# An encoder layer on one core: x loads from two queues, sines behind the Squares, token 512 split once, even sums begun in the second k loop, operand loads behind gate loads

## Chip, cores and metric

The kernel runs on 1 core of one Trainium2 chip. The metric is the device time of one execution in microseconds, given as the median of several runs. A profiled execution has its own time and its own span, which is counted from the first to the last instruction.

## What is computed

Two sequences (x_prompt and x_sample, each 1024 tokens x 1024 channels) go through one layer. Cut to what matters:

```
xn = rmsnorm(x, g_pre);  p = xn @ w_in
fv, fg, hv, hg, mg = split(p)                       # 1024, 1024, 3072, 1024, 2048 columns
fz = fftn(fv as (L, 4 groups, 256), axes=(L, 256)).real
y_f = (fz * silu(fg)) @ w_fourier_out
v, x1, x2 = split(short_conv(hv, w_short))          # width 3 along the sequence
kf = rfft(two-sided filters from a small MLP with two sines)
z = v
for n, gate in enumerate((x1, x2)):
    z = gate * (long_conv(z, kf[:, n]) + hyena_d[n] * z)
y_h = (z * silu(hg)) @ w_hyena_out
g_f, g_h = split(sigmoid(mg + b_merge))
out = (g_f * y_f + g_h * y_h) @ w_out
return x + rmsnorm(out, g_post)
```

Everything is float32. TensorE multiplies rounded operands (F32R), so each operand is split into a rounded part h and a remainder l, and one product is three matmuls: h x h, h x l and l x h (`mm3`). The rounding is a ScalarE cast, the remainder a VectorE (or GpSimd) subtraction; both together are `split`.

## The kernel before

The kernel has four phases in order of time: the Fourier phase (0 to about 225 us), the main phase with filters, input projections and long convolutions (to about 1700 us), the gates, and the output phase (from about 1990 us). Each engine executes its instructions in order. That order comes from a tile scheduler that goes by priorities, by the buffers of the pools (tiles with one tag share `bufs` buffers, and a new tile waits until the readers of the old one are done) and by explicit constraints: `tc.issue_after(ins)` puts what is issued in its block behind the instruction `ins`, where both are on the same engine. DMAs started with `nc.sync`, `nc.scalar` and `nc.gpsimd` are issued from the queues of SyncE (SP), ScalarE (ACT) and GpSimd (POOL).

`phase_fourier` goes through the sequences b = 0 and b = 1.

- `hidden(layer, px, pf)` (L273) computes one layer of the filter network: a matmul `phd`, a chain of VectorE operations that brings the argument into the range of the sine (`sin_of`, L256), two Sin activations on ScalarE, and the store of the result. Layer 0 is called ahead of the first sequence; layer 1, which reads layer 0 back, behind the last half.
- `norm(b, px, pf)` (L303) loads eight tiles x (128 tokens x 1024 channels) on SP, squares each on ScalarE with a row sum, takes the reciprocal root for four tiles at a time in eleven small VectorE operations (`rstd`) and makes four diagonal matrices `dg` from it. For b = 1 it is placed behind the last rounding of the second half's weights (`behind`).
- `xtile(b, k, px, fo)` (L327) is one step of the k loop over the 128-channel blocks: matmuls `tpx` against the diagonals transpose and normalise block k; ScalarE copies them to `xg`, scaled with g_pre; `xg` is stored to `d_x`. VectorE folds the tokens (`eo`, even and odd parts; the odd part of b = 1 is on GpSimd), and `eh`, `el` are their split. Token 512, which has no partner in the fold, is split in every step with two VectorE operations of 128 x 2 (`x5`). Tile xg has two buffers, and GpSimd writes its two last columns with a memset.
- `weights(pw, W, half, k, first)` (L360) loads the block `wfv` of the input projection's Fourier columns on SP, adds and subtracts its halves (`wer`, `wor`) and splits them (`we`, `wo`).
- `pfv(p, e, m, k, W, fo)` is one step over k of sum m of the even (e = 0) or odd (e = 1) part. For b = 0 six of the eight sums of the first half are begun: their PSUM tiles are allocated ahead of the k loop (four in "mm", two in "X"), and every step of the loop adds to them. For b = 1 no sum is begun.
- `fourier_half(b, half, ...)` completes the sums, rounds them (`ee`, `oo`), forms the sums of token 512 (`pfx`, in PSUM "X", then `x5t`), multiplies along the sequence (`stage`: `pse`, `pso`, then `sev`, `sst`, `pp` or `qp`) and along the channels (`pP`, `pQ`, then `fPs`, `fPm`, `fA`, `fB`), and stores to `d_fz`. The halves run in the order (b, half) = (0,0), (0,1), (1,1), (1,0).

Constants: `vec` is loaded on SP, and `seq` (2 MB), `alt`, `chan` and `chx` on POOL, behind a copy that reads the reciprocal roots of the first sequence. `th`, `wsh` and `bm` are loaded on SP at the start of the main phase's code. That code also loads layer 1's result (`hidr`), rounds it on ScalarE and subtracts on VectorE (`hid`, L879 and L880).

In the output phase `project` multiplies 8 operands with weights loaded on POOL. `ahead` loads and rounds an operand for the next of these passes (`operand`, SP, L1126), and `gated` loads a gate (`g`, SP, L1168), opens it with a sigmoid, and multiplies the result with it. Eight steps dt make one pass, and there are two passes (Fourier, long convolution) for each of four units.

The lines of all splits are those of the helpers: L171 (cast), L181 (subtract, add, multiply), L177 (scalar_tensor_tensor), L194 (matmul).

Of the kernel before, what the change touches and what calls it, by code (L numbers as in the profile page):

```python
# [16 lines left out]
P = 128  # L17
# [144 lines left out]
class K:  # L162
# [13 lines left out]
    def stt(self, eng, out, a, s, b, op0=MUL, op1=ADD):  # L176
        self.nc.vector.scalar_tensor_tensor(out, a, s, b, op0=op0, op1=op1)  # L177
# [78 lines left out]
    def sin_of(self, y, k, out, src_ps, f, b):  # L256
# [14 lines left out]
        nc.scalar.activation(out, y, AF.Sin)  # L271

    def hidden(self, layer, px, pf):  # L273
# [14 lines left out]
        else:  # L288
# [5 lines left out]
            y, k = [[t[:, 0:512], t[:, 512:1024]] for t in (y, k)]  # L294
        for n in range(2):
            p = self.psum("mm", 4, "phd")
            nc.tensor.matmul(p, w, z[:, 512 * n:512 * n + 512], start=True, stop=True)
            self.sin_of(y[n], k[n], out[n], p, self.hfb[:, 2 * layer:2 * layer + 1],
                        self.hfb[:, 2 * layer + 1:2 * layer + 2])
        nc.sync.dma_start(self.d_h if layer else self.d_h1, h)  # L300


    def norm(self, b, px, pf):  # L303
# [3 lines left out]
        nc, a = self.nc, self.a  # L307
# [4 lines left out]
        for m in range(8):  # L312
# [4 lines left out]
            nc.sync.dma_start(x, a[f"x{b}"][m * P:(m + 1) * P, :])  # L317
            self.xs.append(x)
            sq = px.tile([P, D], F32, tag="xg", name="sq", bufs=2)
            nc.scalar.activation(sq, x, AF.Square, accum_out=ss[:, m:m + 1])  # L320
            if m % 4 == 3:
                q = slice(m - 3, m + 1)
                self.rstd(px, rs[:, q], ss[:, q], 4)
                for j in range(m - 3, m + 1):
                    nc.vector.tensor_scalar(dg[:, j], self.ident, rs[:, j:j + 1], None, op0=MUL)

    def xtile(self, b, k, px, fo):  # L327
# [11 lines left out]
        for n in range(2):  # L339
# [4 lines left out]
            nc.scalar.activation(xg[:, 512 * n:512 * n + 512], tp, AF.Copy, scale=self.gpre[:, k:k + 1])  # L344
        nc.sync.dma_start(self.d_x[b][k], xg[:, 0:L])
        eo = px.tile([P, 2, 2, 256], F32, tag="eo", name="eo", bufs=2)
# [3 lines left out]
        self.sub("pool" if b else "dve", eo[:, 1], fw, bw)  # L350
        self.split(fo["eh"][:, k], fo["el"][:, k], eo, "dve", "act")
        x5 = fo["x5"][:, k]
        self.split(x5[:, b:b + 33:32], x5[:, 2 + b:35 + b:32], xg[:, 512:513].to_broadcast([P, 2]), "dve", "dve")
# [24 lines left out]
    def pfv(self, p, e, m, k, W, fo):  # L378
        r, c0 = m // 2, P * (m % 2)
        self.mm3(p[:, :(260, 256)[e]], (fo["eh"][:, k, e, r, c0:c0 + P], fo["el"][:, k, e, r, c0:c0 + P]),  # L380
                 (W[e][0][:, k], W[e][1][:, k]), k == 0, k == 7)

    def fourier_half(self, b, half, W, fo, px, pf, begun={}):

        nc = self.nc
# [5 lines left out]
        for e, (W_, n, X_) in enumerate(((WE, 260, EE), (WO, 256, OO))):  # L391
            for m in range(4):
                p = begun.get((e, m))
                if p is None:
                    p = self.psum("mm", 4, f"pfv{e}")
                    for k in range(8):
                        self.pfv(p, e, m, k, W, fo)
                self.split(X_[0][:, m], X_[1][:, m], p[:, :n], "dve", "act")
                if e == (b + half == 0):

                    if m == 0:
                        p5 = self.psum("X", 2, "pfx")[0:36, :260]
# [43 lines left out]
        for g in range(2):  # L446
            cs = slice(130 * g, 130 * g + P)
            PP.append(pair([P, 514], "pp", 2))
            stage(P, lambda m: (EE[0][:, m, cs], EE[1][:, m, cs]), 0, X5[:, cs], PP[g], "TX"[g])
        stage(34, lambda m: (EX[0][:, m], EX[1][:, m]), 0, XX, [PX], "T")  # L450
        for g in range(2):
# [6 lines left out]
            for n in range(2):  # L458
# [14 lines left out]
                nc.scalar.activation(Pm[:, :w], pP, AF.Copy, scale=vec[:, 11:12])  # L473
# [8 lines left out]
                self.stt("dve", B[:, 1024 - t0:1024 - t0 - w:-1], pQ[:, r], vec[:, 12:13], Pm[:, r])  # L482
            nc.gpsimd.dma_start(self.d_fz[b][2 * gg], A[:, 0:1024])
            nc.gpsimd.dma_start(self.d_fz[b][2 * gg + 1], B[:, 0:1024])

    def phase_fourier(self):
        tc, nc, a = self.tc, self.nc, self.a
        with ExitStack() as es:
# [7 lines left out]
            fo["x5"] = pc.tile([P, 8, 36], F32R, name="x5")  # L496
            fo["x5t"] = pc.tile([P, 260], F32R, name="x5t")
# [11 lines left out]
            for b in range(NB):  # L509
                fo["eh"] = pe.tile([P, 8, 2, 2, 256], F32R, tag="eh", name="eh")  # L510
                fo["el"] = pe.tile([P, 8, 2, 2, 256], F32R, tag="el", name="el")
                if b == 0:
                    self.hidden(0, px, pf)
                with tc.issue_after(behind.ins) if b else ExitStack():
                    self.norm(b, px, pf)
                begun = {}
                if b == 0:
                    W = self.open_weights(pw)
                    for e, m in [(0, 0), (0, 1), (0, 2), (0, 3), (1, 0), (1, 1)]:
                        begun[e, m] = self.psum("X", 2, "pfv1") if e else self.psum("mm", 4, "pfv0")  # L520
                for k in range(8):
                    if b == 0:
                        self.weights(pw, W, 0, k, True)
                    self.xtile(b, k, px, fo)
                    for (e, m), p in begun.items():
                        self.pfv(p, e, m, k, W, fo)
                for half in ((0, 1), (1, 0))[b]:
                    if b + half == 0:
                        nc.sync.dma_start(self.vec, a["c_vec"])
                        for t in ("seq", "chan"):  # L530
                            nc.gpsimd.tensor_copy(fo[t][:, 0, 0:1], self.rs[:, 7:8])
                        nc.gpsimd.dma_start(fo["seq"], a["c_seq"])
                        nc.gpsimd.dma_start(fo["alt"], a["c_alt"])
                        nc.gpsimd.dma_start(fo["chan"], a["c_chan"])
                        nc.gpsimd.dma_start(fo["chx"].rearrange("p a b c -> p (a b c)"), a["c_chx"])
                    elif b + half != 2:
# [3 lines left out]
                        behind = self.rounded  # L540
                    self.fourier_half(b, half, W, fo, px, pf, begun)
                    begun = {}
                    if (b, half) == (1, 1):
                        self.hidden(1, px, pf)
# [323 lines left out]
    def phase_main(self, nct=8, nb=NB, nf=16):  # L868
        tc, nc, a = self.tc, self.nc, self.a
        with ExitStack() as es:  # L870
# [8 lines left out]
            nc.scalar.copy(self.hid, hid)  # L879
            self.sub("dve", self.hid[64:128], hid[64:128], self.hid[64:128])  # L880
# [7 lines left out]
            for t, n in ((self.th, "c_th"), (self.wsh, "w_short"), (self.bm, "b_merge")):  # L888
                nc.sync.dma_start(t, a[n])
# [218 lines left out]
    def phase_out(self):  # L1108
# [6 lines left out]
        with ExitStack() as es:  # L1115
# [3 lines left out]
            self.nw = 0  # L1119
# [345 lines left out]
```

## Time and profile before

| | |
|---|---|
| median of 3 runs | 2445.93 us (2445.39 to 2446.81) |
| the profiled execution | 2449.26 us |
| its span | 2447.1 us |
| mean granted TensorE clock | 0.997 |
| VectorE, ScalarE, GpSimd busy | 1893.8, 1096.8, 485.9 us |
| data moved | 429.36 MB, mean 175 GB/s |

In the rows of the profile, "out<-in" are the program's names for the tiles, and L194 and the like are lines of the kernel. A bracket behind a row of the timeline is the idle time of the engine before that instruction and what ended it. "x8" is the number of instructions that a row takes together. A matmul whose operands aren't rounded (`phd`, `tpx`) stands as two in TensorE's rows. The granted clock is 1.00 at full speed.

### The profile page before, as it was taken

What the parts mean: (1) busy time and instruction counts of PE and PEld (TensorE: products, weight loads), DVE (VectorE), ACT (ScalarE), POOL (GpSimd) and SP (SyncE); (2) the same over time, 40 slices, a digit from 0 to 9 for tenths busy, and PEclk for the clock granted to TensorE, in tenths of its full rate; (3) what the DMA queues carried; (4) which work ended last, traced back from release to release, by engine and by line L of the source; (5) the groups of instructions that cost most, each with busy time, mean ns of one, the idle gap of its engine ahead of it and who ended that gap; (6) DMA issues with size and microseconds to landing.
All of it is one profiled execution on the core that took longest, in us unless ns stands there. A gap on an engine that the chain in (4) does not pass through costs nothing.

```text
span 2447.1 us, 36853 instructions
## 1 busy us (share of the span) xinstructions
PE 2396.1 (98%) x13196; PEld 2082.3 (85%) x13196; DVE 1893.8 (77%) x3405; ACT 1096.8 (45%) x2063; POOL 485.9 (20%) x516
## 2 busy tenths in 40 slices
PE   6999999999999999999999999999999999999998
PEld 5988888888888888888888888888788888888886
DVE  7687888888748999999989999766555455665677
ACT  5545677767633433334223333333344444544343
POOL 1341222222143433331000000112200111122111
PEclk9999999999999999999999999999999999999999
DMA  7545655555555555445434444335454567776543
GB/s 273 170 141 191 224 175 173 167 175 167 173 194 177 172 177 173 165 165 192 146 128 134 141 141 138 121 121 184 154 174 159 198 210 255 245 250 213 169 164 129
DMA packets 225151, 429.36 MB, mean 175 GB/s; under 512 B 23542, under 2 KB 87255, under 8 KB 224456
## 3 DMA queue, kind: packets, MB, share of 16 engines
q1 hardware_dynamic: 198444, 333.34, 41.1%
q0 software_dynamic: 26336, 93.65, 10.9%
q8 instruction: 104, 1.70, 0.3%
q14 instruction: 79, 0.65, 0.1%
q10 hardware_dynamic: 188, 0.02, 0.0%
HBM read 290.60 MB, written 136.31 MB: 174 GB/s over the span
## 4 chain that ended last, share of the span: by engine, by line
PE 88%; DMA 5%; issue 3%; DVE 2%; ACT 1%; POOL 1%; SPq 0%; DVEq 0%; POOLq 0%; ACTq 0%
PE pin L194 41%; PE pT L194 7%; PE pg L194 7%; PE pX L194 7%; PE po L194 6%; PE pyh L194 5%; PE pyf L194 5%; PE pXf L194 3%; PE pfv L194 2%; DMA wr<-in_w_fo 1%; PE pft L194 1%; PE tph L792 1%; DMA wr<-in_w_ho 1%; PE tpx L194 1%; DMA wfv<-in_w_fv 1%
## 5 line engine op out<-in xcount | busy, mean ns | idle before, releaser
L194 PE MATMUL pin<-xh,wl 128*128 128x512 f32 x1472 | 577.2, 392 | 2.6 <-POOL wl L181 2.6
L194 PE MATMUL pin<-xl,wh 128*128 128x512 f32 x1472 | 575.6, 391 | 2.4 <-DVE xl L181 2.4
L194 PE MATMUL pin<-xh,wh 128*128 128x512 f32 x1472 | 576.5, 392 | 0.7 <-DMA wh<-d_w 0.7
L181 POOL TENSOR_TENSOR wl<-wr,wh 128x512 fp32r<-128x512 f32 x136 | 240.3, 1768 | 1144.0 <-ACT wh L171 1105.9
L194 PEld LDWEIGHTS pin<-xh,wl 128*128 128x128 f32 x1472 | 277.1, 188 | 54.9 <-POOL wl L181 4.1
L194 PEld LDWEIGHTS pin<-xl,wh 128*128 128x128 f32 x1472 | 277.1, 188 | 54.3 <-DVE xl L181 3.2
L194 PEld LDWEIGHTS pin<-xh,wh 128*128 128x128 f32 x1472 | 277.1, 188 | 52.1 <-DMA wh<-d_w 1.1
L171 ACT CAST wh<-wr 128x512 fp32r<-128x512 f32 x264 | 162.8, 619 | 346.0 <-PE pin L194 136.8
L194 PE MATMUL pT<-cinv,yh 128*128 128x256 f32 x1024 | 193.1, 283 | 0.0
L194 PEld LDWEIGHTS pT<-cinv,yh 128*128 128x128 f32 x1024 | 164.0, 190 | 9.0
L181 DVE TENSOR_TENSOR t<-pX,k 128x1024 f32<-128x1024 f32 x128 | 155.9, 1218 | 10.9 <-PE pX L194 9.3
L194 PE MATMUL pX<-bh,cfwd 128*128 128x256 f32 x768 | 159.6, 286 | 0.0
L181 DVE TENSOR_TENSOR wl<-wr,wh 128x512 fp32r<-128x512 f32 x128 | 87.2, 687 | 93.5 <-ACT wh L171 93.2
L194 PE MATMUL pyf<-sf,wh 128*128 128x512 f32 x512 | 158.0, 390 | 0.9 <-ACT wh L171 0.9
L194 PE MATMUL pyh<-sh,wh 128*128 128x512 f32 x512 | 157.3, 389 | 0.0
L171 ACT CAST bh<-b 128x512 fp32r<-128x512 f32 x144 | 89.0, 620 | 126.7 <-DVE b L181 84.5
L194 PE MATMUL pT<-cinv,yl 128*128 128x256 f32 x512 | 144.9, 283 | 0.0
L171 ACT CAST yh<-y 128x512 fp32r<-128x512 f32 x128 | 79.2, 619 | 114.1 <-DVE y L181 91.3
L194 PEld LDWEIGHTS pX<-bh,cfwd 128*128 128x128 f32 x768 | 126.3, 190 | 2.5
L194 PEld LDWEIGHTS pyf<-sf,wh 128*128 128x128 f32 x512 | 96.0, 188 | 21.3 <-ACT wh L171 1.6
L194 PEld LDWEIGHTS pyh<-sh,wh 128*128 128x128 f32 x512 | 96.1, 188 | 19.9
L194 PE MATMUL pX<-bl,cfwd 128*128 128x256 f32 x384 | 109.6, 285 | 0.0
(354 smaller groups left out, 5262.7 us busy)
## 6 DMA issues: line engine op xcount, KB each, us to landing
k<-d_k SPq DMA_DIRECT2D x128, 512.0 KB, 4.0
wr<-in_w_in SPq DMA_DIRECT2D x136, 256.0 KB, 3.1
d_g<-gt SPq DMA_DIRECT2D x124, 256.0 KB, 2.6
d_k<-kt SPq DMA_DIRECT2D x128, 128.0 KB, 2.1
d_k<-kt SPq DMA_DIRECT2D x64, 256.0 KB, 2.3
wr<-in_w_fo POOLq DMA_DIRECT2D x64, 256.0 KB, 4.0
g<-d_g SPq DMA_DIRECT2D x64, 256.0 KB, 4.2
wr<-in_w_ho POOLq DMA_DIRECT2D x64, 256.0 KB, 3.7
```

The lines of the kernel that those rows point to most:

```text
L171: self.rounded = nc.scalar.copy(h, src)
L181: return e.tensor_tensor(out, a, b, op=op)
L194: return self.nc.tensor.matmul(out, lhsT, rhs, start=start, stop=stop, skip_group_check=shared)
L792: nc.tensor.transpose(tp[:, q * P:(q + 1) * P], eo[:, e, q], self.ident)
```

## The change

The diff, cut to its core:

```diff
@@ sin_of
-        nc.scalar.activation(out, y, AF.Sin)
+        return lambda: nc.scalar.activation(out, y, AF.Sin)
@@ hidden
+        sins = []
...
+            sins.append(self.sin_of(...))
+        def end():
+            for f in sins:
+                f()
+            nc.sync.dma_start(self.d_h if layer else self.d_h1, h)
+        return end
@@ norm(self, b, px, pf, marks)
-            nc.sync.dma_start(x, a[f"x{b}"][m * P:(m + 1) * P, :])
             self.xs.append(x)
+            if b == 0:
+                (nc.scalar if m % 2 else nc.sync).dma_start(x, a[f"x{b}"][m * P:(m + 1) * P, :])
+        for m, x in enumerate(self.xs):
+            if b:
+                nc.sync.dma_start(x, a[f"x{b}"][m * P:(m + 1) * P, :])
             sq = px.tile([P, D], F32, tag="xg", name="sq", bufs=2)
-            nc.scalar.activation(sq, x, AF.Square, accum_out=ss[:, m:m + 1])
+            if b == 0 and m == 7:
+                nc.vector.scalar_tensor_tensor(sq, x, 1.0, x, op0=MUL, op1=MUL, accum_out=ss[:, m:m + 1])
+            else:
+                with tc.issue_after(marks[(0, 0, 0, 1, 1, 1, 2, 2)[m]].ins) if b else ExitStack():
+                    self.squared = nc.scalar.activation(sq, x, AF.Square, accum_out=ss[:, m:m + 1])
@@ xtile
+        nc.scalar.copy(fo["r5"][:, k:k + 1], xg[:, 512:513])
+        if k == 7:
+            r5 = fo["r5"].unsqueeze(2).to_broadcast([P, 8, 2])
+            self.split(fo["x5"][:, :, b:b + 33:32], fo["x5"][:, :, 2 + b:35 + b:32], r5, "dve", "act")
...
-        self.split(x5[:, b:b + 33:32], x5[:, 2 + b:35 + b:32], xg[:, 512:513].to_broadcast([P, 2]), "dve", "dve")
@@ fourier_half
+                    if e + m == 3:
+                        held = self.through
...
-                        p5 = self.psum("X", 2, "pfx")[0:36, :260]
+                        p5 = self.psum(*(("mm", 4) if b + half else ("X", 2)), "pfx")[0:36, :260]
...
-            stage(P, ..., PP[g], "TX"[g])
+            with tc.issue_after(held.ins) if b + half == 0 else ExitStack():
+                stage(P, ..., PP[g], "TX"[g])
@@ phase_fourier
-                with tc.issue_after(behind.ins) if b else ExitStack():
-                    self.norm(b, px, pf)
+                self.norm(b, px, pf, marks if b else None)
+                if b == 0:
+                    with tc.issue_after(self.squared.ins):
+                        end()
...
+                else:
+                    for m in range(2):
+                        begun[0, m] = self.psum("mm", 4, "pfv0")
                 for k in range(8):
                     if b == 0:
-                        self.weights(pw, W, 0, k, True)
+                        with tc.issue_after((self.folded if k else self.scaled).ins), tc.issue_after(self.squared.ins):
+                            self.weights(pw, W, 0, k, True)
                     self.xtile(b, k, px, fo)
+                    if (b, k) == (0, 4):
+                        gate = nc.gpsimd.tensor_copy(fo["seq"][:, 0, 0:1], self.xg[:, 0:1])
+                        with tc.issue_after(gate.ins):
+                            nc.gpsimd.dma_start(fo["seq"], a["c_seq"])
...
+                    if (b, k) == (1, 7):
+                        for m in (2, 3):
+                            begun[0, m] = self.psum("mm", 4, "pfv0")
+                            for j in range(7):
+                                self.pfv(begun[0, m], 0, m, j, W, fo)
...
                         for k in range(8):
                             self.weights(pw, W, half, k, False)
-                        behind = self.rounded
+                            if b == 0 and k in (1, 5):
+                                marks.append(self.rounded)
                     self.fourier_half(b, half, W, fo, px, pf, begun)
+                    if b + half == 0:
+                        marks = [self.odd]
@@ main phase
-            nc.scalar.copy(self.hid, hid)
-            self.sub("dve", self.hid[64:128], hid[64:128], self.hid[64:128])
+            with tc.issue_after(self.third[0].ins), tc.issue_after(self.third[1].ins):
+                nc.scalar.copy(self.hid, hid)
+                self.sub("dve", self.hid[64:128], hid[64:128], self.hid[64:128])
@@ phase_out
                 if dt < 8:
-                    S_.append(operand(i, nm, dt))
+                    with tc.issue_after(self.fetched.ins) if self.fetched else ExitStack():
+                        S_.append(operand(i, nm, dt))
```

In words:

- The x tiles 1, 3, 5 and 7 of the first sequence are loaded from ScalarE's queue. The two sines and the store of layer 0 come behind the last Square on ScalarE; tile 7 is squared on VectorE.
- The weight splits of step k come behind the diagonals (k = 0) or behind the fold of the step before (on VectorE), and behind the last Square (on ScalarE).
- Token 512 is copied by ScalarE in every step (128 x 1) and split once, at k = 7, for all eight steps.
- All eight constants go to POOL's queue, behind a copy that reads `xg` of step 4 of the first sequence: `seq`, `alt`, `chan`, `chx`, `vec`, `th`, `wsh`, `bm`.
- In half (0,0) the first two stages come behind the sum (e, m) = (1, 2). The sums of token 512 use PSUM "mm" in the other halves.
- The Squares of the second sequence are placed behind three marks: tiles 0 to 2 behind the rounding of sum (1, 1) of half (0,0), tiles 3 to 5 behind the rounding of weights k = 1 of half (0,1), and tiles 6 and 7 behind that of k = 5.
- In the k loop of the second sequence, the even sums m = 0 and 1 are added to in every step, and those of m = 2 and 3 catch up at k = 7.
- The rounding of layer 1's result comes behind the last `fB` (VectorE) and `fPm` (ScalarE) of half (1,1).
- In the output phase the load of an operand comes behind the load of the last gate on SP.

55 lines of the change are left out of this document (27 added, 28 removed).

## The prediction

> **What bounds the kernel now.** I read the page first, then a table of stretches, then TensorE's waits, and last the timeline around the long ones.
>
> ```profile
> span 2447.1 us, 36853 instructions
> PE 2396.1 (98%) x13196; PEld 2082.3 (85%) x13196; DVE 1893.8 (77%) x3405; ACT 1096.8 (45%) x2063; POOL 485.9 (20%) x516
> ```
>
> TensorE is busy for 2396.1 of 2447.1 us. The change adds and removes no matmul, so it can only win idle TensorE time, or time in which the clock was low. That is at most 51 us. Where does it lie? In the next view each row is a stretch: its length, then the busy time of each engine, the granted clock and the DMA share.
>
> ```profile
> core 0: us, PE busy (x) PEld busy (x) DVE busy (x) ACT busy (x) POOL busy (x), PEclk, DMA share, GB/s
> 0.00:24.24 24.24, 5.86 (x12) 2.95 (x12) 15.57 (x56) 14.37 (x25) 3.08 (x13) 1.00 0.82 287
> 24.24:62.10 37.86, 35.05 (x264) 34.49 (x265) 30.89 (x70) 22.41 (x37) 4.78 (x10) 0.95 0.77 262
> 62.10:92.13 30.03, 27.49 (x224) 26.64 (x224) 18.75 (x46) 15.36 (x41) 13.71 (x16) 1.00 0.40 124
> 92.13:120.00 27.87, 27.87 (x224) 27.73 (x225) 20.26 (x68) 16.22 (x33) 5.31 (x7) 0.94 0.62 201
> 120.00:144.10 24.10, 19.90 (x163) 18.69 (x162) 22.44 (x40) 15.01 (x24) 13.02 (x14) 1.00 0.75 261
> 144.10:182.00 37.90, 37.90 (x302) 36.10 (x302) 28.15 (x67) 14.64 (x37) 12.50 (x17) 1.00 0.24 85
> 182.00:225.00 43.00, 37.03 (x288) 34.63 (x287) 31.20 (x75) 23.00 (x48) 6.17 (x8) 1.00 0.55 191
> 225.00:1990.00 1765.00, 1759.83 (x9771) 1534.69 (x9771) 1427.89 (x2467) 774.16 (x1461) 341.23 (x299) 1.00 0.49 166
> 1990.00:2437.40 447.40, 445.18 (x1957) 366.34 (x1955) 292.91 (x502) 200.99 (x358) 86.06 (x134) 1.00 0.62 206
> ```
>
> Length less PE busy gives the idle time: 18.4, 2.8, 2.5, 0, 4.2, 0 and 6.0 us in the Fourier phase (33.9 together), 5.2 in the 1765 us behind it, 2.2 in the output phase. Two thirds of all idle time lies in the first tenth of the kernel, and nearly all of the diff is there.
>
> ```profile
> PE tpx L194 <- DMA wfv<-in_w_fv: 9.8, 1, 9.8
> PE tpx L194 <- DVE dg L325: 5.1, 1, 5.1
> PE tpx L194 <- ACT xg L344: 3.5, 2, 2.6
> ...
> PE pso L194 <- DVE sst L181: 2.7, 3, 1.3
> PE pse L194 <- DVE x5t L181: 2.5, 2, 2.1
> PE pP L194 <- issue: 2.3, 1, 2.3
> PE pQ L194 <- DVE fB L177: 2.0, 1, 2.0
> ```
>
> These are TensorE's waits up to 230 us (total, times, longest). The first is put down to a weight load, but tpx reads the diagonals, not wfv: it started at 17.08, behind the first diagonal below. Two gaps cost more than their length:
>
> ```profile
> 93.27:96.68 3.41, 3.41 (x18) 3.41 (x17) 3.21 (x18) 3.24 (x8) 0.00 (x0) 0.50 0.73 259
> ```
>
> Right behind the 2.3 us gap (it ends at 92.13) the granted clock is half for 3.41 us, which loses another 3.41 x 0.5 = 1.7 us. The 2.6 us gap in the first k loop has the same behind it: the clock column from 24 to 62 us is 0.95, and 37.86 x 0.05 is again 1.9. The gaps of 2.0 and 2.1 us between 208 and 217 us were followed by clock 1.00 (row of 182 to 225 us). The point from which a gap costs a half-clock stretch lies here between 2.1 and 2.3 us. [...]
>
> **The change part by part.** The sum is made against the profiled execution, 2449.26 us, 2.2 us around its span; the median of the runs, 2445.93, is 3.33 lower, and I take the same difference off both.
>
> *1. The start.*
>
> ```profile
> 14.56 1.28 ACT L271 ACT_TABLE_LOAD   x1
> ...
> 18.98 1.04 ACT L320 ACTIVATE sq<-x 128x1024 f32<-128x1024 f32 x1
> ```
> ```profile
> 11.46 1.29 DVE L177 SCALAR_TENSOR_TENSOR sq<-sp,sq 128x512 f32<-128x512 f32 x2
> ...
> 16.74 0.87 DVE L325 TENSOR_SCALAR dg<-ident,rs 128x128 f32<-128x128 f32 x4
> 17.86 0.43 DVE L181 TENSOR_TENSOR wer<-wfv 128x260 f32<-128x260 f32 x1 [0.25 <-DMA wfv<-in_w_fv]
> ...
> 20.15 0.17 DVE L242 TENSOR_SCALAR rs_m<-ss 128x4 f32<-128x4 f32 x1 [1.52 <-ACT sq L320]
> ...
> 23.89 0.88 DVE L325 TENSOR_SCALAR dg<-ident,rs 128x128 f32<-128x128 f32 x4
> ```
>
> TensorE runs steadily from 24.24, when the second diagonals start. They follow the last Square (18.98 plus its read, to 20.12), and that came late because ScalarE loaded the Sin table (1.28) and ran two sines between Squares. The reciprocal root then took 20.15 to 23.89, interleaved with weight work on VectorE. In the changed order the sines come behind all Squares, the x tile 7 is squared on VectorE (1.29, from the two half-size ones of that form), and the weight splits come behind the diagonals. x tile 7 lands before 17.86, because wfv, queued behind it, has landed then; I take 17.2 to 17.8. Then 1.29, then the eleven small operations of the root at 0.17 (the first of them, rs_m) and a little between them, 2.2 in all by my estimate, then a quarter of 0.88 for the first diagonal and its hand-over: 21.0 to 21.6. Gain 24.24 - 21.3 = **2.9**. Bounds: 0, if x tile 7 lands as much later as VectorE saves; 4.1, if the root ended where the last Square ended before. The first diagonals stay near 17, so the 9.8 stays. The odd tiles issued from ScalarE count as nothing: the DMA share is already 0.82 over this stretch. Their cost, four DMA issues ahead of ScalarE's first Square, is covered by the 9.9 us for which it was idle here (14.37 busy of 24.24).
>
> *2. First k loop.*
>
> ```profile
> 37.75 1.27 ACT L344 ACTIVATE xg<-tpx,gpre 128x512 f32<-128x512 f32 x2
> 37.78 0.42 DVE L181 TENSOR_TENSOR we<-wer,we 128x260 fp32r<-128x260 f32 x1
> 37.79 0.10 POOL L338 MEMSET xg<- 128x2 f32 x1 [12.32 <-DMA d_x<-xg]
> ```
> ```profile
> L181 DVE TENSOR_TENSOR eo<-xg 128x512 f32<-128x512 f32 x16 | 10.3, 684 | 2.0 <-ACT xg L344 1.4 <-POOL xg L338 0.6
> L181 DVE TENSOR_TENSOR el<-eo,eh 128x1024 fp32r<-128x1024 f32 x8 | 9.7, 1218 | 1.9 <-ACT eh L171 1.9
> L181 DVE TENSOR_TENSOR wer<-wfv 128x260 f32<-128x260 f32 x10 | 4.2, 424 | 2.0 <-DMA wfv<-in_w_fv 2.0
> ...
> L173 DVE CAST x<-xg 128x2 fp32r<-128x2 f32 x8 | 1.8, 221 | 0.0
> L181 DVE TENSOR_TENSOR x<-xg,x 128x2 fp32r<-128x2 f32 x8 | 1.7, 213 | 0.0
> ```
>
> The 2.6 us gap is an xg buffer waiting for its store d_x, issued while the 2 MB of seq were loading; that load now starts behind k = 4, at 21.3 + 4 x 4 = 37 us or so. So 2.6 + 1.7 = 4.3 is free. The new limit is VectorE: two folds (684 ns each), one residue (1218), four weight operations (about 424 each) are 4.3 us a k. Two such operations back to back took 1.29 (the 11.46 row), not 2 x 0.684, so I take 4.0, while TensorE's own work, 35.05 less 1.7, is 4.2 us a k. The 16 operations on token 512 go (1.8 + 1.7 over eight k), against one ScalarE copy a k, beside 22.41 busy of 37.86. TensorE thus stays the bound on average, but pfv follows a chain through VectorE, ScalarE and VectorE again; I leave it 2.6 us of waits. Gain 4.3 - 2.6 = **1.7**; bounds 4.3 (no wait) and -2.1 (VectorE at 5.0 us a k, 8 x 0.8 = 6.4). Eight loads now stand on POOL's queue ahead of the memset of the xg buffer for k = 5; their cover is one k, 4 us, and each us beyond it is lost.
>
> *3. Squares of the second sequence, even sums begun.*
>
> ```profile
> 90.35 1.06 ACT L320 ACTIVATE sq<-x 128x1024 f32<-128x1024 f32 x1 [3.39 <-DMA x<-in_x]
> ```
>
> The 2.3 us "issue" gap is not TensorE's: ScalarE stood at this Square for 3.39 us, and the PSUM evictions behind it on its in-order queue were late. With Squares placed behind rounding of earlier stages, and their loads no longer behind all weight loads, gap and half clock go: 2.3 + 1.7 = 4.0. Against that, two Squares (1.06 each, with their read 1.25) now precede weight casts at the start of the second half: 1.0, bounds 0 and 2.5. Gain **3.0**, bounds 4.0 and 0 (the Square waits at its new place instead). The 4.2 us between 120 and 144 are waits for sst, xg and px while VectorE is 93% busy (22.44 of 24.10). Half of token 512's operations (1.7 us) leave this loop, and two even sums run in it as fill. Gain **2.0**; bounds 4.2 and -3.0. The begun sums hold two of the four "mm" PSUM buffers through this loop, and tpx is left with the other two: a tpx waits for the eviction of the tpx before the last, 1.27 for a pair (the 37.75 row), beside about 3 us a k (eight k in the 24 us), so one late eviction on ScalarE is now felt at once where two were covered before. That is why I take half and not all.
>
> *4. Third half and start of the main phase.*
>
> ```profile
> 213.42 1.22 DVE L181 TENSOR_TENSOR hid<-hidr,hid 64x1024 fp32r<-64x1024 f32 x1
> ```
>
> This operation stands ahead of x5t, for which TensorE waits 2.1 us. Now hid is rounded only behind the half's last sum and pfx is spread among the odd and even sums, so x5t comes earlier: 2.1 off. The taps that read hid come later; the projections fill meanwhile. The 2.0 for fB stays. I take 0.6 back for late taps: gain **1.5**, bounds 4.5 and -2.0.
>
> *5. Output phase.* Operand loads queue on SP behind a gate load, one by one instead of in bursts. Idle is 2.2 us in 447. Gain **0.5**, bounds 2.2 and -2.0.
>
> Sum: 2.9 + 1.7 + 3.0 + 2.0 + 1.5 + 0.5 = 11.6; 2449.26 - 11.6 = 2437.7 in a profiled execution, 2445.93 - 11.6 = **2434.3** as median.
>
> **The rivals.**
>
> *A: the start isn't faster.* Loads from two queues share the same engines, so x tile 7 may land later as the order of tiles gets mixed, and the k loop may be held by VectorE at 4.7 us a k (24.24 + 8 x 4.7 = 62), which ends it where it ended before. For: DMA share 0.82; VectorE 30.89 of 37.86. Against: VectorE loses 3.5 us of work. Items 1 and 2 are nothing: 2445.93 - 7.0 = 2438.9. [...]
>
> *B: the waits of the stages stay.* The longest chain is sum, eviction, sst, rounding, next product, and fill comes too late, so items 3 and 4 give nothing: 2445.93 - 5.1 = 2440.8. For: VectorE 93% busy there. Against: 90.35 is a load's wait and clearly removed.
>
> *C: both*: 2445.4.
>
> *D: slower.* From the second Squares on, the second k loop runs beside the whole chain of the second half, with only two even sums as fill and two buffers for tpx; VectorE's in-order queue holds both. If TensorE then idles as between 120 and 144 us (4.20 of 24.10, 17.4%) in the first k loop and from 92 to 182 us (128 us in all), that is 22.3 us against 7.0 before, a loss of 15.3 against what is left of the gains (2.9, 1.7 of clock in the first loop, 3.0, 1.5 and 0.5: 9.6): 2445.93 + 5.7 = 2451.6. It decides from 13% of idle time there ((9.6 + 7.0) / 128). For: 93%. Against: VectorE is 73% and 74% busy in the neighbouring stretches, which have no idle at all.
>
> **How the numbers follow.** Forecast 0.53, A 0.17, B 0.13, C 0.07, D 0.10. 0.2% (4.9 us) is about what a measurement can tell from no change: faster means below 2441.0. The forecast, most of A and half of B lie there: 0.73. The rest of A and B, with C, is the same: 0.16. D and mishaps: 0.11. The forecast's own range is 2427 to 2441; to hold 8 of 10 it reaches to B and C: 2426 to 2446.5. The low end takes items 1 to 3 at their upper bounds (4.1 + 4.3 + 4.0 + 4.2 = 16.6) and item 4 at 3.
>
> **What would show it.** The second diagonals near 21.3 instead of 23.9; TensorE's first k loop ending near 57.5; no gap over 2.1 us and no half clock before 225 us; no Square waiting for a load at about 86 to 90; VectorE's hid residue behind the last fB sum. It is wrong if a new gap beyond 2.1 us stands before k = 6 or 7 (loads of constants), if the second loop shows TensorE idle above 13%, or if the output phase waits for operands.

## Result and the profile after

The changed kernel takes 2452.99 us (median of 5 runs, 2451.12 to 2456.85), the kernel before 2445.39 (5 runs beside them, 2443.34 to 2446.81). The ratio is 1.0032, 95% interval 1.0022 to 1.0043: 7.6 us slower, where 11.6 us faster were forecast. The profiled execution of the changed kernel took 2452.99 us, with a span of 2451.2.

First the table of stretches of the changed kernel, with the edges that the prediction used for the kernel before (length, then the busy time of TensorE, its weight loads, VectorE, ScalarE and GpSimd, then granted clock, DMA share, GB/s).

```profile
0.00:24.24 24.24, 8.48 (x24) 5.57 (x25) 16.33 (x56) 12.84 (x22) 1.76 (x9) 1.00 0.69 250
24.24:62.10 37.86, 32.74 (x254) 31.55 (x253) 29.39 (x55) 23.57 (x48) 13.14 (x16) 0.95 0.79 277
62.10:92.13 30.03, 26.86 (x199) 25.14 (x199) 19.58 (x60) 17.89 (x45) 11.29 (x17) 0.94 0.60 186
92.13:120.00 27.87, 25.85 (x216) 25.33 (x215) 18.03 (x56) 10.37 (x26) 2.92 (x4) 1.00 0.24 80
120.00:144.10 24.10, 21.55 (x179) 20.66 (x177) 21.49 (x36) 17.01 (x34) 10.68 (x13) 1.00 0.81 276
144.10:182.00 37.90, 36.38 (x284) 33.67 (x283) 24.57 (x49) 15.66 (x37) 12.64 (x16) 1.00 0.31 112
182.00:225.00 43.00, 40.97 (x327) 39.05 (x325) 32.59 (x74) 19.90 (x44) 10.71 (x13) 1.00 0.48 164
225.00:1990.00 1765.00, 1755.80 (x9738) 1529.74 (x9738) 1424.94 (x2467) 775.35 (x1464) 342.80 (x296) 1.00 0.51 165
1990.00:2437.40 447.40, 447.40 (x1975) 370.37 (x1974) 296.99 (x505) 202.59 (x360) 86.36 (x136) 1.00 0.64 208
```

TensorE starts 2.6 us earlier (first row: 8.48 busy for 5.86), and the output phase has no idle time at all (last row: 447.40 of 447.40, 445.18 before). All of this and more is lost from 24 to 120 us, where TensorE's matmul counts fall behind (254 for 264, 199 for 224, 216 for 224), and behind 225 us, where idle time grew from 5.2 to 9.2 us. The longest of its waits up to 230 us (total, times, longest):

```profile
PE tpx L194 <- DVE dg L339: 12.3, 2, 10.1
PE pfv L194 <- ACT eh L171: 4.8, 4, 2.4
PE phd L298 <- DMA hd_w<-in_filt_w: 3.4, 1, 3.4
PE pfv L194 <- DVE el L181: 3.2, 3, 1.3
PE pfv L194 <- DVE we L181: 1.7, 4, 0.8
PE pfv L194 <- DVE ee L181: 1.5, 2, 1.2
PE pQ L194 <- ACT qp L171: 1.5, 1, 1.5
...
```

The wait of before for `x5t` is gone, those for `xg` and `fB` are 0.3 and 0.6 us, and those for `eh`, `el` and `we` are new or longer. Three stretches of half clock follow gaps, near 52, 62 and 284 us:

```profile
52.30:55.70 3.40, 3.40 (x18) 3.40 (x17) 3.40 (x6) 2.75 (x6) 0.00 (x0) 0.50 1.00 412
61.80:65.80 4.00, 3.66 (x19) 3.46 (x18) 2.73 (x11) 4.00 (x11) 0.89 (x1) 0.59 0.15 52
283.60:287.00 3.40, 2.78 (x10) 2.15 (x11) 2.72 (x5) 1.78 (x6) 1.23 (x1) 0.62 0.29 98
```

Idle time, half clock and short waits add up only with one measure for all three. I call it the lost time: the time up to a point, less the sum over all TensorE instructions started so far of the median start-to-start spacing of that kind of instruction in all these traces. It does not depend on the order of the work, so kernels can be compared at the same time of day. The columns are points in us; the rows are worked out from the traces of the kernel before (twice), the changed kernel and two of the experiments below.

```
us                  25     45     65    100    150    200    300   2000   2300
before            20.1   26.9   27.1   31.8   37.3   38.9   45.8   57.1   60.7
before, again     19.5   25.7   26.0   28.3   33.8   35.5   42.4   54.8   59.3
changed           18.6   20.1   28.5   35.7   41.2   45.5   55.1   64.8   64.5
s1_squares_late   18.8   20.3   26.4   27.7   31.2   36.4   44.2   54.6   54.1
c4_const_cinv     18.5   21.9   24.5   26.4   29.9   33.5   40.5   51.0   50.7
```

At 45 us the changed kernel is 6 us ahead. It loses 8.4 us between 45 and 65 (0.2 to 0.3 before), 7.2 between 65 and 100 (2.3 to 4.7 before) and 9.6 between 200 and 300 (6.9 before). Behind 2000 it loses nothing, where the kernel before loses 3.6 to 4.5.

### The profile page after: what moved, and what is told of

Read it like the earlier page. It is cut to its first block, busy times and chain, and to the rows that moved or that the text cites. A ratio compares the mean times of both kernels' runs of the same rounds, so it can differ in the third digit from the quotient of the medians.

```text
span 2451.2 us, 36831 instructions
## 1 busy us (share of the span) xinstructions
PE 2400.0 (98%) x13196; PEld 2084.1 (85%) x13196; DVE 1891.9 (77%) x3377; ACT 1097.2 (45%) x2079; POOL 493.6 (20%) x519
## 3 DMA queue, kind: packets, MB, share of 16 engines
q10 hardware_dynamic: 764, 2.12, 0.2%
## 4 chain that ended last, share of the span: by engine, by line
PE 88%; DMA 1%; DVE 1%; ACT 0%; issue 0%; POOL 0%; DVEq 0%; ACTq 0%; POOLq 0%; SPq 0%
PE pin L194 40%; PE pT L194 7%; PE pyf L194 7%; PE pg L194 7%; PE pyh L194 7%; PE pX L194 7%; PE po L194 6%; PE pXf L194 3%; PE pft L194 1%; PE tph L835 1%; DMA wr<-in_w_in 1%; DMA wr<-in_w_fo 0%; DVE xl L181 0%; DMA xl<-d_x 0%; POOL wl L181 0%
```

## The experiments

Three theories for 45 to 65 us stood first: GpSimd's queue holds the loop (P), VectorE bounds it (V), or the loads of the constants compete with other loads (M). P's chain is plain in the changed kernel's timeline of GpSimd (start, duration, instruction, idle time before it and what ended it):

```profile
37.10 7.58 POOL L559 CAST seq<-xg 128x1 fp32r<-128x1 f32 x1 [0.62 <-ACT xg L358]
44.62 0.53 POOL L562 DMA_DIRECT2D alt<-in_c_alt  x1
...
48.29 0.59 POOL L566 DMA_DIRECT2D bm<-in_b_merge  x1
48.82 0.21 POOL L352 MEMSET xg<- 128x2 f32 x2
```

and of VectorE:

```profile
44.22 0.42 DVE L181 TENSOR_TENSOR wo<-wor,wo 128x256 fp32r<-128x256 f32 x1
49.03 1.29 DVE L181 TENSOR_TENSOR eo<-xg 128x512 f32<-128x512 f32 x2 [4.39 <-POOL xg L352]
```

A copy of one element a partition took 7.58 us, and ended at 44.68, when VectorE had finished its last operation (44.22 + 0.42). Eight issues and a memset follow, and the fold waits 4.39 us for that memset. TensorE's gap of 2.4 us at 49 and the half clock behind it (1.7) come from there: 4.1 of the 8.4 us.

Most of the rest has M's chain. The 2 MB of `seq` were issued at 46.18. The weight load issued at 51.03 (the first of the second half) landed 8.1 us later, where the one issued at 42.18 took 2.8. VectorE waited for it with the residue `el` behind in its queue, and TensorE waited for `el`:

```profile
59.14 0.43 DVE L181 TENSOR_TENSOR wer<-wfv 128x260 f32<-128x260 f32 x1 [1.34 <-DMA wfv<-in_w_fv]
61.21 0.74 PE L194 MATMUL pfv<-we,el 128*128 128x260 f32 x4 [1.34 <-DVE el L181]
```

This is one of three short gaps (0.61, 1.34 and 0.34 us) ahead of the half clock near 62.

**e1_gate_act**

```diff
-                        gate = nc.gpsimd.tensor_copy(fo["seq"][:, 0, 0:1], self.xg[:, 0:1])
+                        nc.scalar.copy(fo["seq"][:, 0, 0:1], self.xg[:, 0:1])
+                        gate = nc.gpsimd.dma_start(fo["seq"], a["c_seq"])
```

> The changed kernel, but the one-element copy that holds the eight constant loads back is made by ScalarE, not GpSimd. Theory P (GpSimd's queue): in the changed kernel that copy took 7.58 us on GpSimd beside a VectorE without idle, and with the eight issues behind it held the memsets of xg until 48.9; the 8.4 us that TensorE loses between 45 and 65 us come from there. Then at most 4.4 us of issues are left ahead of the memsets: loss there below 4 us, median 2447 (2445 to 2449). Theory V (the k loop is bound by VectorE): nothing changes, 2453, the gap near 49 us stays. Theory M (the constants' loads compete with the last weight loads of the loop): not better than 2451, wherever the copy is made.

Measured: 2451.45 us, ratio to before 1.0026 (1.0017 to 1.0036). The loss from 45 to 65 us is 5.4 us for 8.4, and the median falls by 1.5, which the two intervals (1.0022 to 1.0043 for the changed kernel) do not tell from nothing. Both miss what P expected; the median fits M's "not better than 2451". The fold no longer waits for a memset, but the wait that the prediction took off the kernel before is back. `seq` was issued at 38.54, the store of `xg` at 38.86 landed 9.0 us later, and `xg` waited for it; TensorE stood for 1.8 us, with a half clock behind it:

```profile
48.00 1.27 ACT L358 ACTIVATE xg<-tpx,gpre 128x512 f32<-128x512 f32 x2 [4.57 <-DMA d_x<-xg]
```

**e2_memset_dve**

```diff
-        nc.gpsimd.memset(xg[:, L:L + 2], 0.0)
+        (nc.gpsimd if b else nc.vector).memset(xg[:, L:L + 2], 0.0)
```

> The changed kernel, but the memsets of xg in the first k loop are VectorE's, so that nothing of the loop waits behind GpSimd's queue except the reuse of xg by the copy. Theory P: the copy on GpSimd stays some 7 us long, but VectorE's fold no longer waits 4.4 us for a memset; the gap of 2.4 us near 49 with its half clock goes: median 2448 (2446 to 2450). Theory V: 2453 or more (eight more operations on VectorE). Theory M: the weight load of k = 7 still lands 8 us after its issue and the waits near 58 to 62 stay: 2450 to 2453.

Measured: 2452.35 us, 1.0022 (1.0011 to 1.0033). The loss from 45 to 65 is 6.1 us: the wait for the memset is gone, and in its place stand waits for `wo` and `el` (0.66 and 2.06 us, near 50). The weight load issued at 42.48 landed 10.1 us later, beside `seq` (37.89 to 50.43), and VectorE waited 3.8 us for it. Time and chain are M's, not P's.

**e3_const_before**

```diff
-                    if (b, k) == (0, 4):
...
+                    if b + half == 0:
+                        nc.sync.dma_start(self.vec, a["c_vec"])
+                        for t in ("seq", "chan"):
+                            nc.gpsimd.tensor_copy(fo[t][:, 0, 0:1], self.rs[:, 7:8])
...
```

> The changed kernel with the constants loaded where the kernel before loads them. Theory P: the loss of 8.4 us between 45 and 65 goes, but the xg wait for its store (2.6 us and 1.7 of half clock) may come back near 35: median 2448 (2445 to 2450). Theory V: 2453, the loss stays in the loop. Theory M: 2446, since the weight loads of k = 6 and 7 are alone.

Measured: 2452.83 us, 1.0028 (1.0017 to 1.0038). The loss from 45 to 65 is 2.4 us, of the 8.4, and the median is where it was. The stall goes, as P and M have it, and V falls; the time that both expected does not come. Part of the reason is seen: a store of `xg` again meets `seq` early (8.3 us to land), VectorE waits 1.6 us for a weight load there, and TensorE has a gap of 1.8 us at 33 with a half clock behind it, so that by the same measure it is only 2.0 us ahead of the changed kernel at 65. In the profiled execution (2450.92 us) these 2 us last to the end; the median does not show them.

**e4_before_gate**: the kernel before, with the block `if (b, k) == (0, 4)` of the change in place of its own constant loads.

> The kernel before with nothing but the constants moved to GpSimd's queue behind the copy of k = 4. Theory P: it wins the 4.3 us of the xg wait near 36 and loses about 8 behind the copy: 2449 (2447 to 2452), slower than before. Theory V: faster than before, 2441, as VectorE's work is that of before. Theory M: 2447.

Measured: 2448.7 us, 1.0016 (1.0006 to 1.0025): the constants' new way alone makes the kernel before 3.9 us slower, in P's range, but not by P's chain. The copy took 1.14 us, and the next memset came at 46.28. TensorE stood for 3.7 us at 51 because `xg` waited for its store, issued at 43.74 beside `seq` (43.66) and landed 10.1 us later:

```profile
53.97 1.27 ACT L344 ACTIVATE xg<-tpx,gpre 128x512 f32<-128x512 f32 x2 [6.70 <-DMA d_x<-xg]
```

So in these traces the transfers beside `seq` land late (M; a store of `xg` issued at 39.04 in the kernel before took 2.7 us), and moving that load moved the wait of before.

The second set asked for the rest.

**d0_before_again**: the kernel before, unchanged.

> The kernel before, unchanged, in a second profiled execution. Theory N (the profile of before that the prediction was made from was not like the median run): its 2449.26 us were 4 us above the median because of the gap of 2.3 us at 90 us and the half clock behind it; a second profile has neither, TensorE runs through from 62 to 120 us, and the time is 2443 to 2446. Rival: the gap and the half clock stand there again, at 88 to 97 us.

Measured: 2446.66 us, ratio 0.9998 (0.9988 to 1.0008); its profiled execution took 2447.95. TensorE's waits from 60 to 100 us in this second profile of before are these, all of them:

```profile
PE pQ L194 <- ACT qp L171: 1.1, 1, 1.1
PE pfv L194 <- DVE we L181: 0.8, 1, 0.8
```

The gap of 2.3 us at 90, from which the prediction won 4.0 us with its half clock, isn't there. But the execution is only 1.3 us shorter than the first one: a gap of 2.1 us near 205 has a half clock behind it in this profile, and had none in the first. N is right about the gap, and its time came out 2 us too low. The profiles of e4 and b1 below, which have the kernel before's work from 65 to 100 us, don't have the gap either: it stands in one of four.

**s1_squares_late**

```diff
-                            if b == 0 and k in (1, 5):
-                                marks.append(self.rounded)
+                        if b == 0:
+                            marks = [self.rounded] * 3
```

> The changed kernel, but all Squares of the second sequence come behind the last rounding of the second half's weights, as in the kernel before. Theory S (the Squares' new place makes ScalarE late for the weights and sums of the second half): TensorE's loss between 65 and 100 us falls from 7.2 us to below 3, median 2448 (2446 to 2450). Rival G (the begun sums of the second loop): the loss between 65 and 100 stays above 5 and the median at 2452 or more, since the second loop then starts later too.

Measured: 2445.66 us, 1.0002 (0.9992 to 1.0012): 7.3 us less than the changed kernel, equal to the kernel before. The loss between 65 and 100 is 1.3 us. ScalarE's timeline shows it; in the changed kernel, from the first weight cast of the second half to the last:

```profile
71.74 0.72 ACT L171 CAST wo<-wor 128x256 fp32r<-128x256 f32 x2
72.36 1.07 ACT L334 ACTIVATE sq<-x 128x1024 f32<-128x1024 f32 x1
73.32 0.19 ACT L334 ACTIVATION_READ_ACCUMULATOR sq<-x 128x1 f32 x1
73.41 1.05 ACT L334 ACTIVATE sq<-x 128x1024 f32<-128x1024 f32 x1
...
74.45 0.40 ACT L171 CAST we<-wer 128x260 fp32r<-128x260 f32 x1
...
83.00 0.40 ACT L171 CAST wo<-wor 128x256 fp32r<-128x256 f32 x1 [3.57 <-POOL wor L181]
...
85.81 1.06 ACT L334 ACTIVATE sq<-x 128x1024 f32<-128x1024 f32 x1
...
89.61 0.40 ACT L171 CAST wo<-wor 128x256 fp32r<-128x256 f32 x1
```

and with the Squares late:

```profile
69.36 0.71 ACT L171 CAST wo<-wor 128x256 fp32r<-128x256 f32 x2
...
81.53 0.40 ACT L171 CAST wo<-wor 128x256 fp32r<-128x256 f32 x1
81.84 1.06 ACT L334 ACTIVATE sq<-x 128x1024 f32<-128x1024 f32 x1
```

The sixteen casts begin 2.4 us apart and end at 90.0 in the one and at 81.9 in the other, 8.1 us apart, and TensorE's sums of the second half use them one after the other. ScalarE is not busy all the while: at 83.00 it had stood idle for 3.57 us, for a `wor` whose weight load was issued at 77.07. With the Squares late that load was issued at 72.6. Tiles `wfv`, `wer` and `wor` have two buffers each, so a late cast also makes a later load late. This load and the next then took some 5 us to land (2.6 to 3.0 with the Squares late), beside loads of the second sequence's x tiles, which the change moved here too. The two longest of TensorE's waits from 62 to 120 us in the changed kernel are

```profile
PE pfv L194 <- DVE ee L181: 1.5, 2, 1.2
PE pfv L194 <- DVE we L181: 1.4, 3, 0.8
```

and all of them with the Squares late


```profile
PE pfv L194 <- DVE ee L181: 0.3, 1, 0.3
PE pfv L194 <- DVE we L181: 0.2, 1, 0.2
PE pP L194 <- ACT sev L452: 0.2, 1, 0.2
```

**g1_no_begun**: no sums begun in the second k loop.

```diff
-                else:
-                    for m in range(2):
-                        begun[0, m] = self.psum("mm", 4, "pfv0")
...
-                    if (b, k) == (1, 7):
...
```

> The changed kernel without begun sums in the second k loop; all eight sums of the third half are formed behind it, as in the kernel before. Theory G: two of four buffers held and the even sums used up leave nothing to fill the waits of 120 to 150 us and of 180 to 240 us; without it their loss of 5.6 and 7.8 us falls by 4 or more in sum, median 2449 (2447 to 2451). Rival: these sums are the fill of the second loop, and without them it loses more: 2454 or above.

Measured: 2457.83 us, 1.0046 (1.0031 to 1.0061). G falls: the begun sums are worth some 5 us in the changed kernel.

**h1_hid_free**

```diff
-            with tc.issue_after(self.third[0].ins), tc.issue_after(self.third[1].ins):
-                nc.scalar.copy(self.hid, hid)
+            nc.scalar.copy(self.hid, hid)
```

> The changed kernel with the rounding of hid left to the scheduler, as in the kernel before. Theory H (the late hid makes the filter taps late, so that TensorE has used up its other work when the weight load behind cinv takes 13 us, and stands at 281 us): the gap of 2.1 us at 281 and its half clock, 4.7 us in all, go; the wait for x5t near 214 (2.1 us) comes back: median 2450.5 (2448 to 2452). Rival: the stall at 281 comes from the load of cinv alone and stays: 2454 or above.

Measured: 2453.61 us, 1.0035 (1.0024 to 1.0047), no different from the changed kernel. The stall near 281 stays (4.9 us lost from 280 to 290): H falls.

The third set went after the mechanism, and after a version without the costs.

**m1_x1_on_act**

```diff
             if b:
-                nc.sync.dma_start(x, a[f"x{b}"][m * P:(m + 1) * P, :])
+                nc.scalar.dma_start(x, a[f"x{b}"][m * P:(m + 1) * P, :])
```

> The changed kernel, Squares at their new places, but the x tiles of the second sequence are loaded from ScalarE's queue. Theory Q (SP's in-order queue): in the changed kernel the loads of x tiles 3 to 7 stand on SP from 65 to 75 us ahead of the weight loads, each waiting for a buffer that an earlier Square frees, and the weights come late. Off SP, TensorE's loss between 65 and 100 us falls from 7.2 us to below 4, median 2449 (2446 to 2451). Theory A (ScalarE's time for eight Squares of 1.25 us among the weight casts): the loss stays, 2453 or above, as ScalarE now issues eight DMAs as well.

Measured: 2456.01 us, 1.0040 (1.0027 to 1.0053). Q falls: off SP, the weights come no earlier (the fifth weight load of the second half was issued at 78.2, in the changed kernel at 77.1, with the Squares late at 72.6). It leaves the x loads where they are in time, so their part in slow weight loads (4.5 us for the next one) is not tested by it.

**c1_comb_late**: e1, e2 and s1 together.

> The changed kernel with the Squares late, as in s1_squares_late, with the holding copy on ScalarE and with the first loop's memsets on VectorE. If the Squares' place (7.3 us) and the constants' way (1.5 us in the run with ScalarE's copy) are separate costs, 2443 (2441 to 2445), faster than before by 0.1%. If the one hides the other (the loss before 65 us only moves what waits behind it), 2446, as s1_squares_late.

Measured: 2444.45 us, 0.9998 (0.9990 to 1.0007). This is in the first range (2441 to 2445), but 1.2 us below s1 alone, and neither told from s1 nor from the kernel before.

**c2_comb_early**: e1, e2 and m1 together.

> As the kernel c1_comb_late, but with the Squares at the places of the changed kernel and the second sequence's x tiles loaded from ScalarE's queue. Theory Q: 2444 (2441 to 2447). Theory A: 2450 or above.

Measured: 2449.96 us, 1.0018 (1.0010 to 1.0027): 5.5 us behind c1, as A has it; the x loads are early here too.

**b1_before_operands**: the kernel before, with the last hunk of the diff alone.

> The kernel before with nothing but the operand loads of the output phase behind the gate loads. In the ledger of lost TensorE time the kernel before loses 3.5 to 4.4 us between 2000 and 2300 us, and every kernel with the new order loses nothing there. If the order is what does it: 2441.5 (2440 to 2443.5). If the difference came from where the phase starts: 2445, no change.

Measured: 2442.51 us, 0.9989 (0.9980 to 0.9997). The new order of the operand loads wins 2.0 us by itself; its profile loses nothing from 2000 to 2300.

**m2_three_early**

```diff
-                            if b == 0 and k in (1, 5):
-                                marks.append(self.rounded)
+                        if b == 0:
+                            marks += [self.rounded] * 2
```

> The changed kernel, but of the second sequence's Squares only tiles 0 to 2 stay at their new place (ahead of the second half's weights); tiles 3 to 7 come behind the last rounding of these weights. Theory W (the five Squares among the sixteen weight casts, 1.25 us each, make the weights late): TensorE's loss between 65 and 100 us falls from 7.2 us to below 3, median 2446 (2444 to 2448), as with all Squares late. Rival (the first three, which stand ahead of every weight cast): the loss stays above 5, median 2451 or more.

Measured: 2448.87 us, 1.0016 (1.0007 to 1.0024), between the two. The loss from 65 to 100 us is 3.1, between 1.3 (s1) and 7.2. So the five Squares among the casts, with the loads that go with them, cost about 4.1 us (from 2452.99), and the first three, ahead of the casts, about 3.2 (to 2445.66). This split is rough, as its interval meets both neighbours', and by what chain the first three cost time was not followed.

**a1_after_cinv**

```diff
-                    nc.gpsimd.dma_start(self.cinv, a["c_inv"])
+                if 2 <= i < 10:
+                    h, s = (i - 2) // 4, slice((i - 2) % 4 * INVW // 4, ((i - 2) % 4 + 1) * INVW // 4)
+                    with tc.issue_after(self.left.ins):
+                        nc.gpsimd.dma_start(self.cinv[:, h, s], a["c_inv"][:, h, s])
```

> The changed kernel, but the load of cinv (3 MB, first read near 730 us) goes in eight slices over some 280 us, not in one. Theory L (one large load starves the weight loads beside it, and the changed kernel has less other work ready there): the gap of 2.1 us near 281 us and its half clock go, 4.7 us: median 2448.5 (2447 to 2451). Rival (the stall is late rounding, not the load): 2452 to 2454.

Measured: 2451.54 us, 1.0027 (1.0017 to 1.0037). TensorE's longest waits from 225 to 600 us were, in the changed kernel,

```profile
PE pin L194 <- ACT wh L171: 2.1, 1, 2.1
PE pft L194 <- ACT sev L452: 1.0, 1, 1.0
```

where ScalarE itself waited for a weight load that was issued at 269.57, right behind that of cinv (269.20), and landed 13 us later:

```profile
282.87 0.62 ACT L171 CAST wh<-wr 128x512 fp32r<-128x512 f32 x1 [5.55 <-DMA wr<-in_w_in]
```

With cinv in slices the longest is

```profile
PE pin L194 <- POOL wl L181: 1.0, 1, 1.0
```

so L is right about the stall; the median is 0.5 us above L's range and falls by 1.5 us, no more than the intervals leave open. Why this kernel, and not the one before, runs out of other work there was not settled: cinv's load took 12.0 us there, and no stall followed.

**c3_comb_cinv**: c1 with cinv in slices.

> The kernel c1_comb_late (Squares late, holding copy on ScalarE, memsets on VectorE) with cinv in slices. Theory L: c1 lost 5.2 us between 260 and 290 and was equal to the kernel before; without it 2439.5 (2438 to 2442), faster than before by 0.2%. Rival: 2444.

Measured: 2441.46 us, 0.9986 (0.9977 to 0.9994), in L's range.

**c4_const_cinv**: s1, e3 and a1 together.

> The changed kernel with Squares late, the constants where the kernel before loads them, and cinv in slices. The loss up to 65 us should be 1 to 2 us smaller than in c3_comb_cinv, since no late load of constants meets the last weights of the first loop: 2438.5 (2437 to 2441). If the wait of xg for its store comes back instead: 2442.

Measured: 2439.88 us, 0.9979 (0.9971 to 0.9988). This is in the first range. The version beats both kernels: 4.8 us faster than before and 13 than the changed one. Its first loop, in the view of stretches, runs at full clock:

```profile
24.24:62.10 37.86, 33.64 (x273) 32.35 (x273) 31.71 (x65) 24.79 (x52) 6.49 (x8) 1.00 0.78 266
```

## Why the prediction was wrong

*Item 1, the start: right.* 21.3 was forecast for the second diagonals, TensorE's second start is at 21.6 (a wait of 2.2 us from 19.4), against 24.24 in the first profile of before and 23.1 in the second. In the ledger the changed kernel is 5.6 to 6.8 us ahead at 45, so the wait for xg went as well.

*Item 2, the first k loop: two steps failed.* One is "Eight loads now stand on POOL's queue ahead of the memset" and "their cover is one k, 4 us". The eight issues took 4.2 us, but the copy ahead of them took 7.58 where I had counted nothing: 12 us, and they cost 4.1 us of the 8.4 lost from 45 to 65. The other is "So 2.6 + 1.7 = 4.3 is free". It took the wait for the store as ended, but the load of `seq`, moved to step 4, met the later transfers there: a weight load took 8.1 us to land in the changed kernel, stores of `xg` 9.0 and 10.1 in e1 and e4. What I had named as the sign of a wrong prediction, a gap above 2.1 us ahead of k = 6 or 7, stands at 49.0 (2.4 us, half clock behind it). The constants' way costs the kernel before 3.9 us (e4). In the changed kernel, taking it back (e3) brings the early wait back, and the median doesn't move; why none of the 2 us that its profile wins shows there stays open.

*Item 3, the Squares: wrong in sign, and the largest error.* The step is "two Squares ... now precede weight casts ...: 1.0, bounds 0 and 2.5", with a gain of 4.0 against it. Not two but five stand among the casts and three ahead of them; the order of ScalarE's instructions had all eight. Their new place costs 7.3 us (s1), and with the 4.0 that were not there to win this is 11.3 of the error of 19.2 us (from -11.6 to +7.6). Those 4.0: of four profiles one has such a gap. I took one execution's gap for the kernel's. A Square that delays a cast delays the weights of that k, and TensorE's sums go through the weights k by k (waits for `we` and `ee` from 62 to 120 us in the changed kernel, next to none with the Squares late). Two of the weight loads also landed some 2 us later, beside the x loads that moved with the Squares; no run parts this share from that of ScalarE's time. The begun sums, in contrast, do what I took them for (g1).

*Item 4: the waits that I named went, others came.* `x5t` no longer stops TensorE and `fB` hardly, but near 195 `qp` does (1.5 us), and around the stall at cinv's load, which I had not listed, the profile loses 4.7 us (280 to 290). In the medians it is worth 1.5 (a1) to 3.0 us (c1 against c3), each at the edge of the scatter. Another 4.3 us are lost between 225 and 240 (0.1 before). Their cause stays open: they shrink to 1.0 with the Squares late and stay at 4.4 without the change to `hid` (h1).

*Item 5: right in sign, 0.5 forecast, 2.0 measured* (b1). I looked at idle time alone (2.2 us); lost time, with the short waits, was 3.6 to 4.5.

*The rivals.* D came nearest to the time (2451.6), but by luck, as the mechanism is another. In D's stretches TensorE was idle for 11.2 of 128 us, 8.8%, below the 13% from which D was to decide, and what held it was not VectorE in the second loop, whose stretch is better than before (21.55 busy of 24.10 for 19.90), but the new place of the Squares ahead of it. A's limit, VectorE at 4.7 us a k, isn't what held the first loop: VectorE stood idle there for 4.39 us. A's other half, that tile 7 lands later with loads from two queues, did not come in these profiles: it landed at 16.2 us (17.2 before). The two queues did share the 16 DMA engines: from 11 to 15 us SP's queue alone had 102.5% of them in the kernel before (419 GB/s), and in the changed kernel ScalarE's had 60.8 and SP's 41.5% (412 GB/s).

## What to carry to other kernels

When work is moved forward, count every instruction that it puts ahead of each stage on each engine, and ask which casts of that stage the matmuls consume one by one; an engine that is idle on average was no cover here (ScalarE was busy for 17.89 of the 30.03 us from 62.10, and the Squares' place cost 7.3). A gap that is to be won must be in a second profile of the same kernel: the one of 2.3 us at 90 stands in one of four profiles. A large load that is moved can take its cost with it: look for the loads and stores that it will meet at its new place (beside `seq`, a weight load took 8.1 us for 2.8, stores of `xg` 9.0 and 10.1 for 2.7). And an experiment that removes a stall has to be read up to the next one: here three of them (e1 to e3) put another wait in its place, and the time hardly moved.

## What the runs showed of the hardware

A GpSimd copy of 128x1 took 0.185 us in the kernel before (from `rs`). From an `xg` tile it took 7.25 to 8.24 us in seven executions (the changed kernel, s1, g1, h1, m1, m2 and a1). In the changed kernel VectorE ran without a pause beside it, up to 44.64 us, and it ended at 44.68. The same instruction took 1.14 us in e4 and 0.30 us in e2:

```profile
36.08 0.30 POOL L559 CAST seq<-xg 128x1 fp32r<-128x1 f32 x1 [33.46 <-ACT xg L358]
```

What made it long was not shown: no run took VectorE's work away alone.

The prediction let a gap cost a half clock from a length of 2.1 to 2.3 us on. The traces do not bear that out. Gaps of 1.47 us (185, Squares late) and 2.12 us (205, second profile of before) had a half clock behind them, as had three short ones of 0.61, 1.34 and 0.34 us in the 5 us before 62.5 (changed). A gap of 2.07 us (214, first profile of before) had none.

In the changed kernel the stretches of half clock begin at 52.31, 62.55 and 284.41 us and last 3.41 us each; in the 3.41 us ahead of them TensorE was idle for 72, 49 and 65% of the time. In the first profile of before they begin at 38.65 and 93.27, and the shares are 77 and 67%. One more stands at the kernel's end in each (from 2445.05 and 2441.64). What decides between one gap and another was not shown.

The traces have no record of the clock up to 25.0 us in the changed kernel and 28.4 in the first profile of before, so the 1.00 in the first row of the stretches is not measured. The matmuls `tpx` took 421 ns (median) from 17 us to there, as in the half clock from 38.65 (before), and 275 at full clock from 43 to 60.
